# Gate and up: five units instead of three begin early, with the transposes of the third and fourth tiles of tokens behind them in TensorE's order

## The chip, the cores and the metric

One NeuronCore of one Trainium2 chip. The time is device microseconds of one execution of the whole kernel; the median of three runs of the kernel before was 1610.05 us (1607.22 to 1615.42). The traces name the engines PE (TensorE), DVE (VectorE), ACT (ScalarE), POOL (GpSimd) and SP (SyncE, which issues most DMAs).

## What is computed

The reference is a trunk of two layers over 512 tokens of width 1024 in float32. Layer 0 mixes tokens with a two-dimensional neighbourhood attention, layer 1 with three dilated attentions, merged by their softmax denominators. Each mixer, and each SwiGLU behind it, has a normalization ahead and one behind:

```
def swiglu(x, w_gate, w_up, w_down):
    return (jax.nn.silu(x @ w_gate) * (x @ w_up)) @ w_down

for layer in range(DEPTH):
    h = rms_norm(x, norm_mix_pre[layer])
    h = neighbourhood_attention(...) if layer % 2 == 0 else dilated_attention(...)
    x = x + rms_norm(h, norm_mix_post[layer])
    h = rms_norm(x, norm_ffn_pre[layer])
    x = x + rms_norm(swiglu(h, ...), norm_ffn_post[layer])
```

The hidden width of the SwiGLU is 2816: 22 blocks of 128 columns for gate and as many for up.

## The kernel before

Every float32 product is made of three matmuls of rounded halves (`mm3`: high by high L101, high by low L102, low by high L103). A `split` makes the two halves: ScalarE copies the high one (L89), VectorE subtracts to get the low one (L90). Such halves are called `h_a`, `l_a` and so on in the traces.

Large products save an eighth of their multiplications with a scheme of seven products instead of eight. The tokens (four tiles of 128) and the width are halved; seven operands are made of the quarters: X1A, X1B, D1, S2, S4, S3 and X2B. X1A and X1B hold tokens of tiles 0 and 1 alone. The other five need tiles 2 and 3 too: `operands` makes them on GpSimd with four sums a tile (L346, L348, L350, L352), and after each sum `transposed` sends 512 columns through TensorE (four transposes, L322) into one of two `t` banks, from where ScalarE copies the high half (L324) and VectorE subtracts the low half (L325). That L325 frees the bank. `tr_o1_2_3` is the operand 3 (D1) of tile 2 in layer 1; a tile's five transposes come in the order D1, S2, S4, S3, X2B (3, 4, 5, 6, 2).

Between attention and feed-forward stands `out_proj`: for each of the four tiles the output projection (`yo`), the normalization behind it (L359, L360, L306, L308, L366), the one ahead of the feed-forward (`prenorm`: L313, L304, L308 on GpSimd, L315 on VectorE), and the operands. X1A and X1B lie in `rxc`, the other five in `rxa`.

`gate_up` has 22 units, each one block of gate columns with one of up columns (class `Seven`): 84 matmuls of 128x256 into one bank, 12 for each of the seven products. A unit's `first` is the split of its weights a (`l_a`, from `r_gu` or, for units 2 to 4, from `fg`) and the products p1 (X1A) and p2 (X1B); p2's end also starts its `sink` (L558, L559). `third` makes weight sums (L168 and L169 on GpSimd, L170 and L174 on VectorE) and two more splits. `first` of units 0 to 2 is written ahead of the loop; in the loop `run` issues the steps of unit f, `third` of unit f + 1, and p1 and p2 of unit f + 3 in between. The partial gate of a unit is kept in `g_`, a ring of four buffers in the arena `fg`.

Order: a scheduler places the instructions of the whole program on each engine's queue by its own model of their durations; each engine then works strictly in that order and waits on semaphores. `after(i, j)` only forces i behind j on an engine, without a semaphore. So an edit in one place can reorder queues elsewhere. In the kernel before, the scheduler already draws p1 and p2 of units 3 and 4 ahead of unit 0's later products.

One more place matters: the end of the dilated attention. For each pair of heads j, `weights` exchanges softmax statistics between partitions through DRAM: `swapped` writes 8 KB or 4 KB (L919) and reads them back with four DMAs (L921), twice for a pair. Between the two, VectorE and ScalarE form the weights (exponential: L937). The weights scale 16 blocks of probabilities (L1032, eight for each half), which are then transposed (`t1_j`, L1046, copied out by L1047), multiplied with the values (`o1_j`), and enter the output projection. Scores are `sa_j` and `sb_j`, evicted by L953 on VectorE and L954 on ScalarE. SP's queue carries these small DMAs and the output projection's weights (`wo0` to `wo6`, two DMAs of 512 KB each).

Of the kernel before, what the change touches and what calls it, by code (L numbers as in the profile page):

```python
# [17 lines left out]
P = 128  # L18
SEQ = 512
D = 1024  # L20
# [18 lines left out]
def encoder_kernel(ctx: ExitStack, tc: tile.TileContext, a: dict, out: bass.AP):  # L39
    nc = tc.nc  # L40
# [65 lines left out]
    def after(i, j):  # L106

        tc.add_manual_dep(i.ins, j.ins.name,
                          mybir.DependencyInfo(mybir.DependencyClass.NoSync, mybir.DependencyReason.DATA),
                          reason="start flag")  # L110
# [17 lines left out]
    class Seven:  # L128
# [22 lines left out]
            self.i1 = prod(self.left, self.wa, 0, self.xs[X1A], True)  # L151

        def p2(self):
            after(prod(self.right, self.wa, 1, self.xs[X1B], False), self.i1)
            with tc.high_priority(self.urgent):
                self.sink(0, self.left, self.right)

                dve.memset(self.right, 0.0)
# [159 lines left out]
    def transposed(dst, src, name):  # L318

        p = bank("t", f"tr_{name}")  # L320
        for k in range(4):
            pe.transpose(p[:, k * P:(k + 1) * P], src[:, k * P:(k + 1) * P], ident)  # L322
        p3 = p.rearrange("p (k t) -> p k t", k=4)
        act.activation(dst[0], p3, AF.Copy)  # L324
        dve.tensor_sub(dst[1], p3, dst[0].bitcast(F32))  # L325

    def transposed_all(x, h, t, name):
        for hf in range(2):
# [2 lines left out]

    def operands(xs, x, hs, t, rcomb, name):

        def put(i, v):
            transposed(both(xs[i], ALL, ALL, slice(t % 2 * P, t % 2 * P + P)), v, f"{name}_{i}")

        ha, hb = hs[t][:, :512], hs[t][:, 512:]
        if x is not None:
            transposed_all(x, hs[t], t, name)
        elif t < 2:  # L340
            put(X1A, ha)
            put(X1B, hb)
        if t >= 2:
            h1a, h1b = hs[t - 2][:, :512], hs[t - 2][:, 512:]
            d1, s2 = next(rcomb), next(rcomb)
            pool.tensor_sub(d1, ha, hb)  # L346
            put(D1, d1)
            pool.tensor_sub(s2, d1, h1a)  # L348
            put(S2, s2)
            pool.tensor_add(h1b, s2, h1b)  # L350
            put(S4, h1b)
            pool.tensor_sub(h1a, h1a, ha)  # L352
            put(S3, h1a)
            if x is None:
                put(X2B, hb)

    def postnorm_half(hf, sq, y, g, name):
        m, s = small(f"ym{hf}_{name}"), slice(hf * 512, hf * 512 + 512)
# [136 lines left out]
    def out_proj(w, rv, layer, load_x, us, rings, gains):  # L495
        rbig, rhn, rcomb = rings
        g1 = gain(gains[0], a["g_mix_post"][layer])
        g2 = gain(gains[1], a["g_ffn_pre"][layer])
        us = [u for k in range(0, KD, 2) for u in units2(w[k:k + 2], f"wo{k}_{layer}", us[k:k + 2])]
        hs = {}  # L500

        def product(t):
            y = [bank(("pp", "pp", "s", "s", "pp", "o", "pp", "pp")[2 * t + hf], f"yo{layer}_{t}_{hf}")
                 for hf in range(2)]
            for k in range(KD):
                for hf in range(2):
                    mm3(y[hf], both(rv[k], ALL, block(t)), both(us[k], ALL, slice(hf * 512, hf * 512 + 512)),
                        k == 0, k == KD - 1)
            return y

        def post(t, y):
            x, hs[t] = next(rbig), next(rhn)
            load_x(x, t)
            postnorm(hs[t], y, g1, x, f"o{layer}_{t}")
            nc.sync.dma_start(spill[2 * layer][t], x)
            xs_[t] = x

        def pre(t):
            prenorm(hs[t], xs_[t], g2, f"o{layer}_{t}")

        def ops(t):
            operands(xs, None, hs, t, rcomb, f"o{layer}_{t}")

        xs_ = {}
        y0=product(0)
        y1=product(1)
        post(0,y0)
        post(1,y1)
        pre(0)
        pre(1)  # L530
        ops(0)
        ops(1)
        y=product(2)
        post(2,y)
        pre(2)
        y=product(3)
        ops(2)
        post(3,y)
        pre(3)
        ops(3)  # L540

    def gate_up(layer, xs, hid, fg):
        wg, wu = a["wg"], a["wu"]
        raws = ring(fg, 0, 2 * D, 3)
        g_, u_, p5_ = ring(fg, 6 * D, 512, 4), ring(fg, 8 * D, 512, 2), ring(fg, 9 * D, 256, 2)
        v_ = w22_ring(rxc[:, 4 * D:5 * D])
        units, us = {}, {}

        def unit_of(f):
            if f in units or f >= FT:  # L550
                return units.get(f)
            raw = load2((wg[layer, f], wu[layer, f]), f"gu{layer}_{f}", None if f % 5 < 2 else next(raws))
            b, g = bank(("s", "s", "pp", "o", "pp", "pp")[f % 6], f"gu{layer}_{f}"), next(g_)

            def sink(n, left, other):
                u = us.get(f)
                if n == 0:
                    act.activation(g[:, :256], other, AF.Copy)  # L558
                    dve.tensor_add(g[:, :256], g[:, :256], left)  # L559
                elif n == 1:  # L560
                    act.activation(u[:, :256], other, AF.Copy)
                    dve.tensor_sub(u[:, :256], u[:, :256], left)  # L562
                elif n == 2:
                    dve.tensor_sub(u[:, 256:], other, left)
                else:
                    act.activation(g[:, :256], g[:, :256], AF.Silu)
                    act.activation(g[:, 256:], left, AF.Silu)
                    dve.tensor_mul(hid[f], *(v.rearrange("p (h c) -> p h c", h=2) for v in (g, u)))

            units[f] = Seven(raw, b, xs, f"{layer}_{f}", sink, None, next(v_), (pool, pool, dve, dve))  # L570
            return units[f]

        ahead = 3
        for f in range(ahead):
            unit_of(f).first()
        for f in range(FT):
            for i in range(f, min(f + 2, FT)):
                if i not in us:
                    us[i], units[i].p5 = next(u_), next(p5_)
            run(unit_of(f), unit_of(f + 1), unit_of(f + ahead))  # L580

# [179 lines left out]
    def mix_out(layer, w, rxb, load_x):  # L763
        for j in range(PAIRS - 1):
            nc.gpsimd.dma_start(rxa[:, j * D:(j + 1) * D], rvd[layer][j])
        us = [None] * 4 + [hl(rxa, 8, D)] + [hl(rxb, 2 * i, D) for i in range(3)]
        with arena(f"ep{layer}", 12 * D, "right") as ep:
            out_proj(w, rv, layer, load_x, us, (ring(ep, 0, D, 4), ring(ep, 4 * D, D, 4), ring(ep, 8 * D, 512, 4)),
                     (ep[:, 10 * D:11 * D], ep[:, 11 * D:12 * D]))

    def ffn(layer, stack):
        hl_ = ring(rxc, 0, D, 5)
        rxb = None
        with arena(f"hid{layer}", FT * 512, "right") as hm:
            h2 = hm.rearrange("p (h x) -> p h x", h=2)
            hid = [h2[:, :, f * 256:f * 256 + 256] for f in range(FT)]
            with arena(f"fg{layer}", 9 * D + 512) as fg:
                gate_up(layer, xs, hid, fg)
            with arena(f"ed{layer}", D, "right") as ed, arena(f"yp{layer}", 2 * D, "right") as yp:
                rcomb = ring(ed, 0, 512, 2)  # L780

                def sink(t, xt, hs, gn):
                    if layer == 1:
                        for n in range(2 if t == NT - 1 else 1):
                            s = slice(512 * n, 512 * n + 512) if t == NT - 1 else ALL
                            (nc.sync, act)[n].dma_start(out[t][:, s], xt[:, s])
                    else:
                        nc.sync.dma_start(spill[1][t], xt)
                        prenorm(hs[t], xt, gn, f"n{layer}_{t}")
                        operands(mixer_operands(rxb) if rxb is not None else None, x, hs, t, rcomb, f"n{layer}_{t}")  # L790

                with arena(f"wd{layer}", 2 * QF) as mem, arena(f"raw{layer}", 2 * D) as more:
                    end = down(layer, hm, hl_, mem, yp, more, sink)
                if layer == 0:
                    rxb = stack.enter_context(arena("rxb1", 6 * D, dtype=F32R))
                end()
        return rxb
# [66 lines left out]
             lambda v: v.rearrange("p (i c) -> p c i", i=ROWS))  # L864

    inner.close()
    mix_out(0, a["na_o"], rxb, lambda xt, t: nc.sync.dma_start(xt, a["x_rows"][t]))
    stack.close()
    rxb = ffn(0, stack)

# [255 lines left out]
                nc.sync.dma_start(xt[32 * r + 16:32 * r + 32], rows[r, 0:16])  # L1128

    inner.close()  # L1130
    mix_out(1, a["dil_o"], rxb, load_block)
    stack.close()
    ffn(1, stack)


def _blocks(w, cols):
# [79 lines left out]
```

## Time and profile before

| | us |
|---|---|
| median of three runs | 1610.05 |
| the profiled execution, its time | 1605.1 |
| its span in the trace | 1603.3 |
| TensorE busy | 1486.7 |
| VectorE busy | 1205.0 |
| ScalarE busy | 897.6 |
| GpSimd busy | 628.1 |

The granted clock of TensorE was 0.976 on the mean. A row of waits reads: engine, line and tile that waited, what released it, microseconds in total, times, the longest. A row of a timeline reads: start, duration, engine, line, operation, tile out <- tiles in, shapes, count, and in brackets the idle time before it with what ended it. A row of stretches reads: from and to, length, then the busy time of PE, weight loads, DVE, ACT and POOL with the number of instructions, the granted clock, the DMA share and GB/s. A row of DMAs reads: what, queue, number, KB each, microseconds from issue to landing.

### The profile page before, as it was taken

The page shows a single profiled execution, that of the slowest core. Times are in us where ns is not written, and L with a number is a line of the kernel's source. Part 1 is how long each engine was busy: PE and PEld are TensorE (multiplying, and loading weights), DVE is VectorE, ACT ScalarE, POOL GpSimd, SP SyncE. Part 2 cuts the span into 40 slices and gives each one's busy share as a digit, 9 for nine tenths or more (in the row PEclk, how much of TensorE's full clock was granted, in tenths as well). Part 3 has the DMA queues.
Part 4 walks back from the last instruction along what each step waited for, and adds up shares of the span by engine and source line. Part 5 has one row for each costly group of instructions (what it writes and reads, how often), then busy time and mean ns, then how long its engine had stood idle before and what let it go on. Part 6 is the DMA issues. An engine that isn't in the chain of part 4 may idle for free.

```text
span 1603.3 us, 28068 instructions
## 1 busy us (share of the span) xinstructions
PE 1486.7 (93%) x10788; PEld 1366.7 (85%) x10788; DVE 1205.0 (75%) x1884; ACT 897.6 (56%) x1787; POOL 628.1 (39%) x500
## 2 busy tenths in 40 slices
PE   7999898899999898889999999999887899999896
PEld 7988776899999786879999988988766899999774
DVE  5488966799998867677677776776536699998866
ACT  5367753555555556434467776676654555555554
POOL 3356434533330222566555443544104533330221
PEclk9999999999999999999999999999998999999999
DMA  4323455133323995534322322322626133323993
GB/s 171 109 80 105 150 191 197 66 106 106 106 80 99 256 243 172 173 132 159 109 95 62 121 81 92 133 67 61 222 88 197 66 106 106 106 80 102 265 244 112
DMA packets 77766, 208.99 MB, mean 130 GB/s; under 512 B 18560, under 2 KB 28800, under 8 KB 77632
## 3 DMA queue, kind: packets, MB, share of 16 engines
q1 hardware_dynamic: 65456, 165.11, 30.5%
q0 software_dynamic: 12032, 41.82, 10.9%
q8 instruction: 85, 1.39, 0.4%
q14 instruction: 49, 0.40, 0.1%
q10 hardware_dynamic: 144, 0.26, 0.0%
HBM read 185.04 MB, written 22.12 MB: 129 GB/s over the span
## 4 chain that ended last, share of the span: by engine, by line
PE 61%; DVE 12%; DMA 11%; issue 6%; ACT 5%; POOL 4%; SPq 1%; POOLq 0%; DVEq 0%; ACTq 0%
PE gu L101 9%; PE gu L102 9%; PE gu L103 9%; PE pp_d L101 4%; PE pp_d L102 3%; PE pp_d L103 3%; DMA raw<-wd 3%; DMA wd<-wd 2%; PE t L1046 2%; PE sb L986 1%; ACT ap L1032 1%; PE vd L102 1%; PE vd L101 1%; PE vd L103 1%; PE yd_pp L101 1%
## 5 line engine op out<-in xcount | busy, mean ns | idle before, releaser
L103 PE MATMUL gu<-rxc,l_a 128*128 128x256 f32 x352 | 102.0, 290 | 3.3 <-DVE l_a L90 3.3
L102 PE MATMUL gu<-rxc,h_a 128*128 128x256 f32 x352 | 102.4, 291 | 0.0
L101 PE MATMUL gu<-rxc,h_a 128*128 128x256 f32 x352 | 102.1, 292 | 0.1
L101 PE MATMUL gu<-rxa,h_c 128*128 128x256 f32 x352 | 100.2, 285 | 0.7 <-DVE fg L562 0.4
L101 PE MATMUL gu<-rxa,h_b 128*128 128x256 f32 x352 | 99.7, 284 | 0.7 <-ACT rxa L324 0.7
L102 PE MATMUL gu<-rxa,h_b 128*128 128x256 f32 x352 | 99.8, 284 | 0.0
L103 PE MATMUL gu<-rxa,l_c 128*128 128x256 f32 x352 | 99.6, 283 | 0.0
L102 PE MATMUL gu<-rxa,h_c 128*128 128x256 f32 x352 | 99.6, 283 | 0.0
L103 PE MATMUL gu<-rxa,l_b 128*128 128x256 f32 x352 | 99.5, 283 | 0.0
L604 POOL DMA_DIRECT2D wd<-wd x36 | 34.3, 995 | 137.8 <-DVE l_d0p L90 49.7
L168 POOL TENSOR_TENSOR fg<-fg 128x512 f32<-128x512 f32 x24 | 39.8, 1659 | 120.9 <-DVE l_a L90 119.7
L954 ACT ACTIVATE ap<-ap 128x256 f32<-128x256 f32 x128 | 63.9, 502 | 31.4 <-DVE ap L953 30.8
L168 POOL TENSOR_TENSOR r_d<-r_d 128x512 f32<-128x512 f32 x24 | 39.7, 1656 | 105.9 <-DVE l_ad L90 97.7
L168 POOL TENSOR_TENSOR r_gu<-r_gu 128x512 f32<-128x512 f32 x20 | 35.5, 1773 | 115.8 <-DVE l_a L90 115.8
L89 ACT ACTIVATE rxc<-hid 128x512 fp32r<-128x512 f32 (+1 forms) x84 | 49.2, 591 | 54.1 <-PE yd_s L102 33.6
L103 PEld LDWEIGHTS gu<-rxc,l_a 128*128 128x128 f32 x352 | 70.0, 199 | 3.7 <-DVE l_a L90 3.7
L101 PEld LDWEIGHTS gu<-rxc,h_a 128*128 128x128 f32 x352 | 69.8, 199 | 0.6 <-ACT rxc L324 0.6
L102 PEld LDWEIGHTS gu<-rxc,h_a 128*128 128x128 f32 x352 | 70.0, 199 | 0.0
L101 PEld LDWEIGHTS gu<-rxa,h_c 128*128 128x128 f32 x352 | 67.5, 192 | 1.7 <-DVE fg L562 1.5
L101 PEld LDWEIGHTS gu<-rxa,h_b 128*128 128x128 f32 x352 | 67.6, 193 | 1.0 <-ACT rxa L324 1.0
L102 PEld LDWEIGHTS gu<-rxa,h_c 128*128 128x128 f32 x352 | 67.5, 192 | 0.2
L103 PEld LDWEIGHTS gu<-rxa,l_b 128*128 128x128 f32 x352 | 67.6, 192 | 0.0
(599 smaller groups left out, 6265.2 us busy)
## 6 DMA issues: line engine op xcount, KB each, us to landing
r_d<-dil_qk SPq DMA_DIRECT2D x48, 512.0 KB, 4.5
r_d<-wd SPq DMA_DIRECT2D x30, 512.0 KB, 4.4
wd<-wd POOLq DMA_DIRECT2D x30, 512.0 KB, 10.4
fg<-wg SPq DMA_DIRECT2D x24, 512.0 KB, 3.7
fg<-wu SPq DMA_DIRECT2D x24, 512.0 KB, 4.6
r_gu<-wg SPq DMA_DIRECT2D x20, 512.0 KB, 3.7
r_gu<-wu SPq DMA_DIRECT2D x20, 512.0 KB, 4.6
r_n<-na_qk SPq DMA_DIRECT2D x16, 512.0 KB, 4.5
```

Source lines behind the costliest of these rows:

```text
L89: act.activation(h, src, AF.Copy)
L101: i = pe.matmul(o, s[0], m[0], start=start, stop=False, skip_group_check=True)
L102: pe.matmul(o, s[0], m[1], start=False, stop=False, skip_group_check=True)
L103: pe.matmul(o, s[1], m[0], start=False, stop=stop, skip_group_check=True)
L168: e[0].tensor_add(q[0], q[0], q[2])
L604: nc.gpsimd.dma_start(v, src, accum_op=ALU.add)
L954: act.activation(pr[:, f], pr[:, f], AF.Exp, bias=st[:, c:c + 1], scale=-1.0, accum_out=st[:, c + 2:c + 3])
L986: pe.matmul(ss[hd][:, f0:f0 + P], qf[rw, block(c)], kf[rw, block(c)], start=True, stop=True)
L1032: act.activation(v, v, AF.Copy, scale=w[:, 2 * b + hd:2 * b + hd + 1])
L1046: pe.transpose(t[:, block(i)], part(a_b, *blocks[4 * n + i]), ident)
```

## The change

`first` of five units instead of three is written ahead of the loop, and the loop starts a later unit only from unit 5 on. `operands` returns the first transpose of each operand, and `gate_up` forces those of tile 2 behind the start of unit 1's second product and those of tile 3 behind that of unit 4. The ring `g_` has five buffers, and the arena is 512 columns wider. The returned lists are passed through `out_proj`, `mix_out` and `ffn`.

```diff
         def p2(self):
-            after(prod(self.right, self.wa, 1, self.xs[X1B], False), self.i1)
+            self.i2 = prod(self.right, self.wa, 1, self.xs[X1B], False)
+            after(self.i2, self.i1)
...
         for k in range(4):
-            pe.transpose(p[:, k * P:(k + 1) * P], src[:, k * P:(k + 1) * P], ident)
+            i = pe.transpose(p[:, k * P:(k + 1) * P], src[:, k * P:(k + 1) * P], ident)
+            first = i if k == 0 else first
...
+        return first
...
+        trs = []
+
         def put(i, v):
-            transposed(both(xs[i], ALL, ALL, slice(t % 2 * P, t % 2 * P + P)), v, f"{name}_{i}")
+            trs.append(transposed(both(xs[i], ALL, ALL, slice(t % 2 * P, t % 2 * P + P)), v, f"{name}_{i}"))
...
         y=product(3)
-        ops(2)
-        post(3,y)
+        trs = ops(2)
+        post(3, y)
         pre(3)
-        ops(3)
-
-    def gate_up(layer, xs, hid, fg):
+        return trs, ops(3)
+
+    def gate_up(layer, xs, hid, fg, trs):
         wg, wu = a["wg"], a["wu"]
         raws = ring(fg, 0, 2 * D, 3)
-        g_, u_, p5_ = ring(fg, 6 * D, 512, 4), ring(fg, 8 * D, 512, 2), ring(fg, 9 * D, 256, 2)
+        g_, u_, p5_ = ring(fg, 6 * D, 512, 5), ring(fg, 8 * D + 512, 512, 2), ring(fg, 9 * D + 512, 256, 2)
...
-        ahead = 3
-        for f in range(ahead):
+
+
+        ahead, early = 3, 5
+        for f in range(early):
             unit_of(f).first()
+        for f, v in zip((1, early - 1), trs):
+            for tr in v:
+                after(tr, units[f].i2)
         for f in range(FT):
...
-            run(unit_of(f), unit_of(f + 1), unit_of(f + ahead))
+            run(unit_of(f), unit_of(f + 1), unit_of(f + ahead) if f + ahead >= early else None)
...
-            with arena(f"fg{layer}", 9 * D + 512) as fg:
-                gate_up(layer, xs, hid, fg)
+            with arena(f"fg{layer}", 10 * D) as fg:
+                gate_up(layer, xs, hid, fg, trs)
```

How the queues stand then, at the places of which the prediction speaks. Lines of the changed kernel are a few higher for the same operation (L168 becomes L169, L346 to L352 become L351 to L357, L325 becomes L327, L937 becomes L948, L1032 becomes L1043).

On TensorE, layer 0 changes little: the first transposes of tile 2 move behind 12 matmuls each of units 0 and 1, and those of tile 3 by a few matmuls. In layer 1 tile 2's first and second transposes move behind 35 matmuls of units 0 and 1, and the third of tile 2 behind all of unit 2; the 22 matmuls of unit 4 that stood between the third and fourth transposes of tile 3 now stand ahead of them.

GpSimd's queue at the change to the feed-forward in layer 1, before (`fg1` are the weight sums of units 2 to 4, two for each unit; `rs_o1_3` is tile 3's factor in the normalization; `ep1` the sums for tile 3's operands):

```order
L168 TENSOR_TENSOR fg1_12636<-fg1_12636 128x512
L169 TENSOR_TENSOR fg1_12636<-fg1_12636 128x512
L308 TENSOR_TENSOR rs_o1_3_12585<-v_o1_3_12583,mhalf_71 128x1
L346 TENSOR_TENSOR ep1_12186<-ep1_12186 128x512
L168 TENSOR_TENSOR fg1_12636<-fg1_12636 128x512
L348 TENSOR_TENSOR ep1_12186<-ep1_12186 128x512
L169 TENSOR_TENSOR fg1_12636<-fg1_12636 128x512
L350 TENSOR_TENSOR ep1_12186<-ep1_12186 128x512
L352 TENSOR_TENSOR ep1_12186<-ep1_12186 128x512
```

and now:

```order
L169 TENSOR_TENSOR fg1_12636<-fg1_12636 128x512
L309 TENSOR_TENSOR rs_o1_3_12585<-v_o1_3_12583,mhalf_71 128x1
L170 TENSOR_TENSOR fg1_12636<-fg1_12636 128x512
L169 TENSOR_TENSOR fg1_12636<-fg1_12636 128x512
L351 TENSOR_TENSOR ep1_12186<-ep1_12186 128x512
L170 TENSOR_TENSOR fg1_12636<-fg1_12636 128x512
L169 TENSOR_TENSOR fg1_12636<-fg1_12636 128x512
L353 TENSOR_TENSOR ep1_12186<-ep1_12186 128x512
L170 TENSOR_TENSOR fg1_12636<-fg1_12636 128x512
L355 TENSOR_TENSOR ep1_12186<-ep1_12186 128x512
L357 TENSOR_TENSOR ep1_12186<-ep1_12186 128x512
```

Unit 4's two sums, which stood behind all of tile 3's, now stand ahead of the third. In layer 0 the same two move in, and one sum of unit 3 goes ahead of tile 3's factor.

VectorE's queue there, now (before, `l_b1_0` and the two L325 of tile 2 stood ahead of L315, and unit 4's split far behind it):

```order
L372 SCALAR_TENSOR_TENSOR ep1_12186<-ep1_12186,rs_yo1_3_12577 128x1024
L90 TENSOR_TENSOR l_a1_2_12711<-fg1_12636,h_a1_2_12710 128x1024
L305 TENSOR_SCALAR v_o1_3_12583<-m_o1_3_12581 128x1
L90 TENSOR_TENSOR l_a1_3_12745<-fg1_12636,h_a1_3_12744 128x1024
L316 SCALAR_TENSOR_TENSOR ep1_12186<-ep1_12186,rs_o1_3_12585 128x1024
L90 TENSOR_TENSOR l_a1_4_12779<-fg1_12636,h_a1_4_12778 128x1024
L565 TENSOR_TENSOR fg1_12636<-fg1_12636,gu1_0_12640 128x256
L327 TENSOR_TENSOR rxa_76<-tr_o1_2_3_12527,rxa_76 128x4x128
L327 TENSOR_TENSOR rxa_76<-tr_o1_2_4_12535,rxa_76 128x4x128
```

The splits of units 3 and 4 moved ahead, and the subtractions that free the banks of tile 2's first transposes moved behind them.

SP's queue at the end of the dilated attention, before (`sw0` and `sw2` are pair 6's two swaps, `r_wo2_1` to `r_wo6_1` the output projection's weights):

```order
L919 DMA sw0_6472<-ap1_6470 128x16
L85 DMA r_wo2_1_12200<-dil_o 128x1024 x2
L921 DMA ap1_6470<-sw0_6472 32x4x4 x4
L919 DMA sw2_6474<-ap1_6470 128x8
L921 DMA ap1_6470<-sw2_6474 32x4x2 x4
L85 DMA r_wo4_1_12211<-dil_o 128x1024 x2
```

and now:

```order
L85 DMA r_wo2_1_12200<-dil_o 128x1024 x2
L930 DMA sw0_6472<-ap1_6470 128x16
L932 DMA ap1_6470<-sw0_6472 32x4x4 x4
L85 DMA r_wo4_1_12211<-dil_o 128x1024 x2
L930 DMA sw2_6474<-ap1_6470 128x8
L932 DMA ap1_6470<-sw2_6474 32x4x2 x4
```

Each of the two weight loads moved ahead of the small write of its swap. On ScalarE the exponential of pair 6's weights and both groups of eight scalings moved behind splits of the output projection's weights, and the second group behind two copies of pair 7's queries (L425 and L426 before).

More of the change, by code (lines that the diff above doesn't have):

```diff
@@ L355, in operands @@
                 put(X2B, hb)
+        return trs
     def postnorm_half(hf, sq, y, g, name):
@@ L521, in ops @@
         def ops(t):
-            operands(xs, None, hs, t, rcomb, f"o{layer}_{t}")
+            return operands(xs, None, hs, t, rcomb, f"o{layer}_{t}")
         xs_ = {}
@@ L767, in mix_out, with ffn @@
         with arena(f"ep{layer}", 12 * D, "right") as ep:
-            out_proj(w, rv, layer, load_x, us, (ring(ep, 0, D, 4), ring(ep, 4 * D, D, 4), ring(ep, 8 * D, 512, 4)),
+            return out_proj(w, rv, layer, load_x, us, (ring(ep, 0, D, 4), ring(ep, 4 * D, D, 4), ring(ep, 8 * D, 512, 4)),
                      (ep[:, 10 * D:11 * D], ep[:, 11 * D:12 * D]))
-    def ffn(layer, stack):
+    def ffn(layer, stack, trs):
         hl_ = ring(rxc, 0, D, 5)
@@ L866, in encoder_kernel @@
     inner.close()
-    mix_out(0, a["na_o"], rxb, lambda xt, t: nc.sync.dma_start(xt, a["x_rows"][t]))
+    trs = mix_out(0, a["na_o"], rxb, lambda xt, t: nc.sync.dma_start(xt, a["x_rows"][t]))
     stack.close()
-    rxb = ffn(0, stack)
+    rxb = ffn(0, stack, trs)
     ap = inner.enter_context(arena("ap1", 14 * D + 3264, "right"))
@@ L1130, in encoder_kernel @@
     inner.close()
-    mix_out(1, a["dil_o"], rxb, load_block)
+    trs = mix_out(1, a["dil_o"], rxb, load_block)
     stack.close()
-    ffn(1, stack)
+    ffn(1, stack, trs)
 def _blocks(w, cols):
```

## The prediction

> **What bounds the kernel now.** I read the page first, then TensorE's busy time in stretches, then its waits at the two changes from attention to feed-forward, then the rows there.
>
> ```profile
> span 1603.3 us, 28068 instructions
> PE 1486.7 (93%) x10788; PEld 1366.7 (85%) x10788; DVE 1205.0 (75%) x1884; ACT 897.6 (56%) x1787; POOL 628.1 (39%) x500
> 250.00:312.00 62.00, 50.20 (x311) 44.78 (x310) 47.17 (x59) 30.40 (x58) 38.72 (x26) 0.92 0.41 156
> 350.00:400.00 50.00, 50.00 (x419) 50.00 (x418) 46.58 (x59) 25.77 (x44) 16.32 (x9) 1.00 0.32 106
> 1150.00:1190.00 40.00, 37.35 (x233) 30.24 (x232) 22.46 (x62) 23.70 (x62) 4.66 (x6) 1.00 0.45 155
> 1222.00:1275.00 53.00, 40.46 (x274) 37.72 (x272) 38.70 (x52) 26.27 (x47) 35.47 (x23) 0.87 0.37 136
> ```
>
> TensorE is busy 93% of the span. In the steady part of gate and up (350 to 400) it is busy 50.00 of 50.00 us: a fifth gate buffer and a different interleaving of units can gain nothing there. At the change to the feed-forward it is idle 62.00 - 50.20 = 11.8 us in layer 0 and 53.00 - 40.46 = 12.5 us in layer 1. Only those are there to be won. They split up so (first layer 0, then layer 1):
>
> ```profile
> PE tr_o L322 <- DVE rxc L325: 6.1, 2, 3.5
> PE gu L103 <- DVE l_a L90: 3.3, 2, 2.9
> PE tr_o L322 <- DVE rxa L325: 1.6, 3, 1.0
> ...
> PE tr_o L322 <- DVE rxc L325: 7.7, 2, 4.3
> PE tr_o L322 <- POOL ep L350: 2.8, 1, 2.8
> PE tr_o L322 <- POOL ep L348: 1.4, 1, 1.4
> PE tr_o L322 <- DVE rxa L325: 0.4, 1, 0.4
> ```
>
> The larger halves, 6.1 and 7.7 us, are waits for VectorE to finish the operands of tiles 0 and 1 (rxc is X1A and X1B). Their two parts are the one before tile 1's own transposes and the one before the first transposes of tile 2. In layer 0 the rest hangs on a weight split (l_a), in layer 1 on GpSimd's sums for tile 3.
>
> **The change, part by part.** *The first transposes of tile 2 go behind unit 1's second product.* The wait that stands before them:
>
> ```profile
> 277.42 1.09 PE L322 MATMUL tr_o<-ident,ep 128*128 128x128 f32 x4 [3.55 <-DVE rxc L325]
> 1238.88 1.09 PE L322 MATMUL tr_o<-ident,ep 128*128 128x128 f32 x4 [3.41 <-DVE rxc L325]
> 1238.06 1.27 DVE L325 TENSOR_TENSOR rxc<-tr_o,rxc 128x512 fp32r<-128x512 f32 x2
> ```
>
> What takes their place is gate and up's L102, high weights times the low half of X1A, and the low half of tile 1 is written by the same L325: 1238.06 plus half of 1.27 is 1238.7. So 3.55 and 3.41 us of wait stay, under another name. The gain is four transposes that no longer run at the slow clock, 1.09 against 0.60 us when warm: at most 0.5 us a layer, and I count it as 0, since the same four are paid for later.
>
> *Unit 4's products and splits come earlier, tile 3's chain later (layer 0).* What can go there is the wait for unit 4's split:
>
> ```profile
> 297.68 0.58 PE L103 MATMUL gu<-rxc,l_a 128*128 128x256 f32 x1 [2.88 <-DVE l_a L90]
> 301.87 1.03 PE L322 MATMUL tr_o<-ident,ep 128*128 128x128 f32 x8
> 288.67 2.20 POOL L346 TENSOR_TENSOR ep<-ep 128x512 f32<-128x512 f32 x1 [1.40 <-DVE ep L315]
> 290.83 2.28 POOL L168 TENSOR_TENSOR fg<-fg 128x512 f32<-128x512 f32 x1
> 293.06 1.28 POOL L348 TENSOR_TENSOR ep<-ep 128x512 f32<-128x512 f32 x1
> 294.29 2.25 POOL L169 TENSOR_TENSOR fg<-fg 128x512 f32<-128x512 f32 x1
> 296.51 2.26 POOL L350 TENSOR_TENSOR ep<-ep 128x512 f32<-128x512 f32 x1
> ```
>
> Removing it would bring TensorE to tile 3's second and third transposes (301.87) 2.9 us earlier, at 299.0. But they need L348 and L350, and GpSimd now does one weight add (L168 of unit 3) before tile 3's rstd, and unit 3's L169 and unit 4's L168 and L169 before L348. Of these, L168 and L169 of unit 3 already stood before L350; unit 4's two are new in front of it. Two adds at 1.28 to 2.28 us move L350's end from 298.77 to between 301.3 and 303.3. The earlier matmuls then wait there: the layer 0 sum is between -2.0 (the adds fill the 1.40 us idle before L346: 301.3 - 1.4 = 299.9) and +1.5 (303.3 against 301.87). I take 0, between ends nearly alike.
>
> *The same in layer 1.* Here the order really puts tile 3's transposes behind unit 4, where 22 of its matmuls stood between the third and the fourth.
>
> ```profile
> 1246.70 1.29 POOL L169 TENSOR_TENSOR fg<-fg 128x512 f32<-128x512 f32 x1
> 1249.90 2.20 POOL L346 TENSOR_TENSOR ep<-ep 128x512 f32<-128x512 f32 x1 [1.40 <-DVE ep L315]
> 1252.06 2.42 POOL L168 TENSOR_TENSOR fg<-fg 128x512 f32<-128x512 f32 x1
> 1256.77 1.27 POOL L169 TENSOR_TENSOR fg<-fg 128x512 f32<-128x512 f32 x1
> 1258.00 2.28 POOL L350 TENSOR_TENSOR ep<-ep 128x512 f32<-128x512 f32 x1
> 1260.33 1.12 PE L322 MATMUL tr_o<-ident,ep 128*128 128x128 f32 x4 [2.81 <-POOL ep L350]
> 1265.38 0.60 PE L322 MATMUL tr_o<-ident,ep 128*128 128x128 f32 x4
> ```
>
> GpSimd does unit 4's two adds before L350 too, 2 x 1.27 = 2.5 to 2.42 + 2.25 = 4.7 us, less the 1.40 us that it idled before L346 where that can be used: L350 ends 1.1 to 4.7 us later. I take 4.2, near the slow end, because VectorE's queue now holds the two-input operations L366, three l_a splits and L315 in a row, with the L325 of tile 2 behind them, and GpSimd's adds beside such operations are the ones of 2.2 to 2.4. So tile 3's third transposes move from 1260.33 to 1264.5, the fourth need L352 (one more such add of 1.27, so 1265.8) and start 0.4 later than the 1265.38 of before, although 22 fewer matmuls lie between. Behind an idle stretch the clock is low:
>
> ```profile
> 1261.00:1264.00 3.00, 3.00 (x18) 3.00 (x17) 0.96 (x2) 0.90 (x2) 2.92 (x3) 0.57 0.02 5
> ```
>
> 18 matmuls in 3.0 us, 0.167 each at a granted clock of 0.57, against 50.00 / 419 = 0.119 when warm. The slow stretch now falls on some 12 to 20 matmuls behind the transposes as it fell on others before, but later by the same shift: about +1. The term is +1.5, between -3 (GpSimd not later, 22 matmuls ahead of it) and +4. Before that a new wait stands at tile 2's third transposes: the L325 that frees their bank is behind L315, l_a of unit 4 and L559. It is hidden by the later one as long as it is under some 3 us.
>
> The Trainium skill, "SBUF — State Buffer", section "Who interferes with whom", says that a VectorE operation with two SBUF inputs and a GpSimd operation that reads SBUF block each other for a whole instruction. The trace agrees: 1.27 alone, 2.42 beside such work. By that rule every added pair costs its full length, L350 would be 4.7 late and this term +2.0 instead of +1.5; if the rule did not hold, -3.
>
> *The end of the dilated attention (layer 1) is ordered anew too.* The diff does not touch it, but the scheduler does. On SP's queue the loads of wo2 and wo4 (1 MB each) now stand before the small writes that start the two swaps of pair 6's softmax weights; on ScalarE the exponential of these weights (L937) moves behind two weight splits, and both scalings (L1032, eight each) behind it, the second behind the copies L425 and L426.
>
> ```profile
> ap<-sw SPq DMA_DIRECT2D x4, 2.0 KB, 5.7
> ap<-sw SPq DMA_DIRECT2D x4, 1.0 KB, 1.7
> sw<-ap SPq DMA_DIRECT2D x1, 4.0 KB, 1.4
> 1148.06 9.12 SPq L85 DMA_DIRECT2D r_wo<-dil_o  x4
> 1149.70 3.30 ACT L1032 ACTIVATE ap<-ap 128x256 f32<-128x256 f32 x8
> 1157.96 0.63 ACT L426 ACTIVATE rxc<-ap 64x512 fp32r<-64x512 f32 x1
> 1155.42 0.66 PE L1046 MATMUL t<-ident,ap 128*128 128x128 f32 x4 [1.95 <-ACT ap L1047]
> ```
>
> The first swap's read-back stood behind 1 MB and took 5.7 us; the second's, with nothing ahead, 1.7. So 1 MB ahead costs 4.0. For the first swap the load moves from behind its write to ahead of it: no change. For the second, wo4 (issued at 1148.06, behind it) now stands ahead: +4.0. The second eight scalings, 3.30 us, now follow L426 instead of running before 1153: +3.3. Together pair 6's transposes are 7.3 later. TensorE's order puts 33 output-projection matmuls ahead of all but the first of them, but these are taken from behind, where they covered the evictions of pair 7's scores (between its second and third block of scores stood 18, now none). Cover is moved, not made; TensorE has 40.00 - 37.35 = 2.65 us of idle time in this stretch that moved work could fill, half of it say: 7.3 - 1.3 = 6.0. The bounds are 0 (the 33 matmuls cover all) and 7.3. Pair 7's swaps follow the evictions, and the last output projection waits for pair 7, so the delay comes out at the end.
>
> *The rest* (one more ring buffer, a wider arena, returned lists) issues nothing. The weight loads of units 2 to 4 stand where they stood on SP's queue.
>
> **Sum:** 0 + 1.5 + 6.0 = +7.5. On the profiled execution 1605.1 + 7.5 = 1612.6; the median of the runs shown is 4.95 above that execution, so 1610.05 + 7.5 = 1617.5 us.
>
> **Rivals.** *The change does what it says* (faster): the waits on POOL and on l_a go, 3.3 in layer 0 and 4.2 in layer 1, with 0.5 a layer for warm transposes, and the tail's new order costs nothing since the 33 matmuls cover it: 1610.05 - 8.5 = 1601.5. For it: TensorE has all of units 3 and 4 ahead of tile 3. Against: GpSimd's queue, which these waits end on, only got longer. Chance 0.22.
>
> *Nothing but shifting* (within the bound): layer 1 gives back what it gains and the tail is half covered, 0 + 0 + 3 = 1613. For it: no work is added, and TensorE has filler in each place. Against: the filler in each place is taken from another. Chance 0.32.
>
> *The same losses, larger* is part of my forecast: tail 7.3, layer 1 +4 and layer 0 +1.5 give 1622.9.
>
> The clock makes a rival of size, not of sign: after 2.81 us of waiting in layer 1 the granted clock was 0.57. The Trainium skill, "TensorE: Matmul & The Clock Gate", section "What's actually happening", has the clock halved after an idle window of some 3.4 us. By it, new waits shorter than that would leave the clock high and layer 1 would cost about 1 less; the trace is harsher than that.
>
> **How the numbers follow.** My forecast, slower by about 5 to 13 us, has 0.46; the rivals 0.32 and 0.22. A measurement of this kernel tells about 0.5%, 8.05 us, from no change. My sum of 7.5 lies just under that, with a long side above it (12.8 with the terms' upper ends), and the profile shows no term that would hold the loss down, while the middle case and the lower part of mine fall within the bound: slower 0.46, same 0.32, faster 0.22. The range takes in the faster case down to about 7 us and the larger losses with 6 us for a place that I did not see: 1603 to 1629; mine alone, 1614 to 1624.
>
> **What would show it.** In the changed kernel: TensorE's wait of about 3.4 us on L325 before gate and up's second matmul (first step); tile 3's transposes in layer 0 waiting for L350 with l_a's 2.88 gone; L350 in layer 1 later by 1 to 5 us measured from unit 0's first matmul, and a new wait at tile 2's third transposes; pair 6's second swap with a landing of over 5 us, and more than 2.65 us of TensorE idle between pair 6's and pair 7's scores. I am wrong if steady gate and up is no longer at 50 of 50, if the tail's idle time is as before, or if L348 and L350 end no later.

## The result, and the profile after

| | us |
|---|---|
| kernel before, median of 12 runs | 1608.84 (1605.40 to 1615.42) |
| changed kernel, median of 12 runs | 1609.99 (1606.67 to 1615.12) |
| ratio, 95% interval | 1.0004 (0.9992 to 1.0016) |
| profiled execution of the changed kernel, span | 1607.5 |

The change makes no difference that can be measured; the interval reaches from 1.3 us faster to 2.6 us slower. Forecast was +7.5.

TensorE's busy time of the changed kernel in the same four stretches as before:

```profile
250.00:312.00 62.00, 51.93 (x305) 46.43 (x304) 49.88 (x61) 30.65 (x59) 39.61 (x26) 0.86 0.43 165
350.00:400.00 50.00, 50.00 (x419) 50.00 (x418) 43.67 (x57) 25.66 (x46) 16.64 (x11) 1.00 0.31 106
1150.00:1190.00 40.00, 35.52 (x207) 28.52 (x207) 19.08 (x56) 24.06 (x64) 3.39 (x6) 0.96 0.42 133
1222.00:1275.00 53.00, 40.31 (x259) 36.99 (x258) 40.93 (x49) 24.61 (x44) 36.25 (x23) 0.84 0.34 129
```

The steady part is full as before. At the change in layer 0 TensorE is busy 1.73 us more than before (51.93 against 50.20), and yet does 305 matmuls in place of 311: the column behind the counts of GpSimd, the granted clock, fell from 0.92 to 0.86. Busy time rose because the same work ran slower. Its waits there, first layer 0 (245 to 330), then layer 1 (1222 to 1330):

```profile
PE tr_o L323 <- DVE rxa L327: 4.6, 3, 3.6
PE gu L102 <- DVE rxc L327: 3.2, 1, 3.2
PE tr_o L323 <- DVE rxc L327: 2.3, 1, 2.3
...
PE tr_o L323 <- DVE rxa L327: 4.8, 4, 2.2
PE gu L102 <- DVE rxc L327: 3.8, 1, 3.8
PE tr_o L323 <- DVE rxc L327: 3.7, 1, 3.7
```

Most of the waiting that the change was to end has come back under another name. The wait on l_a (3.3) is gone in layer 0, and the transposes wait 4.6 for the L327 that frees their bank, against 1.6 before. The waits on GpSimd (4.2) are gone in layer 1, and there too 4.8 stand at the banks, against 0.4. The wait for X1A went from the transposes to `gu L102`, about as long as before (3.2 and 3.8 against 3.55 and 3.41).

To compare without the rest of the program I take the stretch from unit 0's first matmul to the end of gate and up's last in one profile. For the changed kernel's layer 1 it is read so:

```profile
1233.40 0.80 PE L101 MATMUL gu<-rxc,h_a 128*128 128x256 f32 x2
...
1485.18 0.28 PE L103 MATMUL gu<-rxa,l_c 128*128 128x256 f32 x1
```

1485.46 - 1233.40 = 252.06 us. The tail of attention is read from layer 1's first output-projection matmul to unit 0's first. All kernels, in us:

| kernel | layer 0 | tail | layer 1 | ratio of times, 95% interval |
|---|---|---|---|---|
| before | 250.21 | 99.33 | 249.12 | 1 |
| changed | 250.16 | 99.38 | 252.06 | 1.0004 (0.9992 to 1.0016) |
| e1: five gate buffers alone | 250.19 | 99.27 | 248.64 | 1.0007 (0.9994 to 1.0019) |
| e2: change in layer 1 alone | 250.72 | 100.20 | 250.82 | 1.0020 (1.0006 to 1.0034) |
| e3: change in layer 0 alone | 250.61 | 100.02 | 249.71 | 1.0007 (0.9995 to 1.0018) |
| e4: tile 2's place alone | 249.92 | 99.20 | 251.12 | 1.0018 (1.0005 to 1.0031) |
| e5: five units early, no place forced | 250.17 | 98.65 | 246.62 | 0.9992 (0.9978 to 1.0006) |
| e9: early, tile 3's place forced | 250.32 | 99.45 | 248.69 | 0.9992 (0.9977 to 1.0007) |
| e6: GpSimd's sums of units 2 on behind | 248.08 | 96.46 | 247.78 | 0.9991 (0.9980 to 1.0003) |
| e8: the sums of units 3 on behind | 250.16 | 98.99 | 245.68 | 0.9982 (0.9970 to 0.9994) |
| e7: change, with e6's sums | 247.79 | 99.52 | 248.35 | 0.9983 (0.9969 to 0.9997) |
| e10: e5 with e6's sums | 247.84 | 97.93 | 245.49 | 0.9957 (0.9942 to 0.9972) |
| e11: e5 with e8's sums | 248.45 | 98.48 | 248.20 | 0.9985 (0.9972 to 0.9999) |

A ratio compares many runs of a kernel with runs of the kernel before beside them; a stretch is read from one profile. How exact a stretch is can be seen where TensorE's order is the same to a matmul or two: layer 0 differs by 0.5 us (e1 and e2), layer 1 by 1.1 (e1 and e3) and 1.2 (changed and e2), the tail by 2.9 (before and e6).

### The profile page after: what moved, and what is told of

It reads as the page before. It is cut to its first block, busy times and chain, and to the rows that moved or that the text cites. A ratio compares the mean times of both kernels' runs of the same rounds, so it can differ in the third digit from the quotient of the medians.

```text
span 1607.5 us, 28077 instructions
## 1 busy us (share of the span) xinstructions
PE 1491.8 (93%) x10788; PEld 1371.3 (85%) x10788; DVE 1189.5 (74%) x1884; ACT 895.8 (56%) x1787; POOL 609.8 (38%) x500
## 4 chain that ended last, share of the span: by engine, by line
PE 59%; DVE 12%; DMA 11%; issue 7%; ACT 5%; POOL 4%; SPq 1%; POOLq 0%; DVEq 0%; ACTq 0%
PE gu L101 9%; PE gu L102 9%; PE gu L103 9%; PE pp_d L101 4%; PE pp_d L102 3%; PE pp_d L103 3%; DMA wd<-wd 2%; PE t L1057 2%; DMA r_d<-wd 2%; DMA raw<-wd 1%; PE sb L997 1%; PE vd L102 1%; ACT ap L1043 1%; PE yd_pp L101 1%; PE yd_pp L102 1%
## 5 line engine op out<-in xcount | busy, mean ns | idle before, releaser
L102 PE MATMUL gu<-rxc,h_a 128*128 128x256 f32 x352 | 102.3, 291 | 7.0 <-DVE rxc L327 7.0
L102 PE MATMUL gu<-rxa,h_b 128*128 128x256 f32 x352 | 101.3, 288 | 0.0
L102 PE MATMUL gu<-rxa,h_c 128*128 128x256 f32 x352 | 99.6, 283 | 0.0
L169 POOL TENSOR_TENSOR fg<-fg 128x512 f32<-128x512 f32 x24 | 36.0, 1500 | 121.8 <-DVE l_a L90 120.6
L169 POOL TENSOR_TENSOR r_d<-r_d 128x512 f32<-128x512 f32 x24 | 39.8, 1658 | 104.8 <-DVE l_ad L90 96.4
L169 POOL TENSOR_TENSOR r_gu<-r_gu 128x512 f32<-128x512 f32 x20 | 29.4, 1470 | 128.9 <-DVE l_a L90 128.9
L102 PEld LDWEIGHTS gu<-rxc,h_a 128*128 128x128 f32 x352 | 69.8, 198 | 7.5 <-DVE rxc L327 7.5
L101 PEld LDWEIGHTS gu<-rxa,h_b 128*128 128x128 f32 x352 | 68.9, 196 | 0.7 <-ACT rxa L326 0.7
L102 PEld LDWEIGHTS gu<-rxa,h_b 128*128 128x128 f32 x352 | 69.0, 196 | 0.0
L101 PEld LDWEIGHTS gu<-rxa,h_c 128*128 128x128 f32 x352 | 67.5, 192 | 1.1 <-DVE fg L568 0.9
```

The costliest lines, as they stand in the source:

```text
L101: i = pe.matmul(o, s[0], m[0], start=start, stop=False, skip_group_check=True)
L102: pe.matmul(o, s[0], m[1], start=False, stop=False, skip_group_check=True)
L169: e[0].tensor_add(q[0], q[0], q[2])
```

## The experiments

**e1, the tail by itself.** Five buffers alone make the scheduler reorder the end of the dilated attention as in the changed kernel (SP's queue is the same; some of pair 7's scores and of pair 6's transposes stand a little elsewhere). Both changes to the feed-forward stay as they were within a matmul; later, where TensorE is full, the units interleave otherwise.

```diff
-        g_, u_, p5_ = ring(fg, 6 * D, 512, 4), ring(fg, 8 * D, 512, 2), ring(fg, 9 * D, 256, 2)
+        g_, u_, p5_ = ring(fg, 6 * D, 512, 5), ring(fg, 8 * D + 512, 512, 2), ring(fg, 9 * D + 512, 256, 2)
...
-            with arena(f"fg{layer}", 9 * D + 512) as fg:
+            with arena(f"fg{layer}", 10 * D) as fg:
```

> The kernel before with five gate buffers instead of four and the wider arena, nothing else. Its queues at both changes to the feed-forward stand within one matmul as before, but the end of the dilated attention is ordered as in the changed kernel (wo2 and wo4 ahead of the small swap writes, L1032 later). So it prices that tail alone. By the prediction's term the tail costs 6.0 us, between 0 and 7.3: ratio 1.0037. By the theory formed from the changed kernel's trace the output projection's matmuls, drawn ahead, cover the later transposes, and the second swap is not later at all: 0 within 1.5 us, ratio 0.999 to 1.001, and TensorE's waits from 1110 to 1222 us sum to within 1.5 us of the 10.3 us of before.

The tail took 99.27 us against 99.33. The ratio is the stronger evidence: 1.0007, with 1.0019 or 3.1 us as its upper end, so 6.0 us is ruled out. TensorE's waits between 1110 and 1222 us, before and in e1:

```profile
PE t L1046 <- ACT ap L1032: 2.7, 1, 2.7
PE yo L101 <- ACT h_wo L89: 2.0, 1, 2.0
PE t L1046 <- ACT ap L1047: 1.9, 1, 1.9
PE sb L986 <- ACT ap L412: 1.3, 1, 1.3
```

```profile
PE t L1046 <- ACT ap L1032: 4.5, 2, 2.6
PE pp_d L101 <- DVE ap L409: 1.3, 1, 1.3
PE yo L101 <- DVE ap L953: 0.9, 1, 0.9
...
PE sa L969 <- DVE ap L953: 0.5, 1, 0.5
```

With the smaller rows 10.3 us became 9.1. The later scalings cost a new wait of 2.6 on L1032 at pair 6's transposes, while pair 7's shrank from 2.7 to 2.0 (4.5 - 2.7 = 1.8 in all), the scores 0.5; the wait on wo0's split (2.0) is gone, and that on pair 6's copies shrank from 1.9 to 0.2.

**e2 and e3, one layer each.**

```diff
-        ahead, early = 3, 5
+        ahead, early = 3, 5 if layer == 1 else 3
...
-        for f, v in zip((1, early - 1), trs):
+        for f, v in zip((1, early - 1), trs if layer == 1 else ()):
```

> The change in layer 1 alone (layer 0 starts three units early, no transposes forced). If layer 1's change to the feed-forward costs about 3 us, as one profile showed (2.9 from unit 0's first matmul to the last of gate and up), the ratio is 1.001 to 1.003 and that stretch is 251 to 253 us against 249.1 before. If the 2.9 was a variation of one profile, the stretch is 249 to 250. The prediction's term was +1.5.

> The change in layer 0 alone. By the prediction's term and the trace of the changed kernel layer 0 is worth 0: the stretch from unit 0's first matmul to the last of gate and up stays 250.2 us within 0.5, ratio 0.999 to 1.001 (the tail's order is the new one too). If the change itself gains there and something else gave it back, the stretch is 2 to 3 us shorter.

Layer 1 alone: 250.82 us, slower by 1.7 than before, and the only half whose time is slower beyond its interval (1.0006 to 1.0034); the changed kernel, with the same layer 1, is not (1.0004). 250.82 is just under the 251 expected, so the 2.9 of the first profile was partly its own. Layer 0 alone: 250.61, nothing beyond the 0.5 that equal orders differ by.

**e4, e5 and e9, the change in its parts.** e4 forces only tile 2's transposes behind unit 1, with three early units:

```diff
-        ahead, early = 3, 5
+        ahead, early = 3, 3
...
-        for f, v in zip((1, early - 1), trs):
-            for tr in v:
-                after(tr, units[f].i2)
+        for tr in trs[0]:
+            after(tr, units[1].i2)
```

> Only tile 2's transposes forced behind unit 1's second product, three units early as before, nothing for tile 3. GpSimd's queue then does not have unit 4's sums ahead of tile 3's third. If the loss in layer 1 comes from pushing tile 2's transposes (their banks are freed late behind L315 and the splits on VectorE), the stretch of layer 1 is 251 to 253 us here too. If it comes from unit 4's earlier splits and sums on VectorE and GpSimd, it is 248 to 249.5.

e5 has five early units and forces nothing; e9 forces only tile 3's transposes:

```diff
-        for f, v in zip((1, early - 1), trs):
-            for tr in v:
-                after(tr, units[f].i2)
```

```diff
-        for f, v in zip((1, early - 1), trs):
-            for tr in v:
-                after(tr, units[f].i2)
+        for tr in trs[1]:
+            after(tr, units[early - 1].i2)
```

> Five units begin early and the ring has five buffers, but no transpose is forced behind anything. Unit 4's splits and sums stand early on VectorE and GpSimd as in the change; in layer 1 tile 2's transposes stay about where they were. If layer 1's loss is the forced place of tile 2's transposes (e4 lost 2.0 with that alone), the stretch of layer 1 from unit 0's first matmul to the last of gate and up is 249 to 250 us and the ratio 0.999 to 1.001. If it is the earlier splits and sums, the stretch is 251 to 253 and the ratio about 1.002.

> The change without the forced place of tile 2's transposes; tile 3's stay forced behind unit 4. If layer 1's loss is tile 2's place alone, layer 1's stretch is 246 to 248 us as in e5 (246.6) and the ratio 0.998 to 1.000. If tile 3's place counts too, it lies between e5's 246.6 and the changed kernel's 252.1, at 249 or more.

In layer 1 tile 2's forced place alone costs 2.0 us (e4, 251.12 against 249.12), five early units alone win 2.5 (e5, 246.62), which is more than either theory gave them; tile 3's place gives 2.1 of that back (e9, 248.69, between the two expectations, and less than twice the 1.2 that equal orders differ by), tile 2's the rest (changed, 252.06, and e2, 250.82). In layer 0 none of the parts moves anything. In e5 layer 1 looks so:

```profile
1249.41 0.60 PE L323 MATMUL tr_o<-ident,ep 128*128 128x128 f32 x4
1251.03 0.60 PE L323 MATMUL tr_o<-ident,ep 128*128 128x128 f32 x4
1256.01 0.63 PE L323 MATMUL tr_o<-ident,ep 128*128 128x128 f32 x4 [1.41 <-DVE rxa L327]
...
1265.66 0.66 PE L323 MATMUL tr_o<-ident,ep 128*128 128x128 f32 x4 [0.16 <-POOL ep L355]
1268.15 0.63 PE L323 MATMUL tr_o<-ident,ep 128*128 128x128 f32 x4 [1.42 <-DVE rxa L327]
```

and in the changed kernel so:

```profile
1252.04 0.63 PE L323 MATMUL tr_o<-ident,ep 128*128 128x128 f32 x4 [1.48 <-DVE rxa L327]
...
1261.59 1.30 PE L323 MATMUL tr_o<-ident,ep 128*128 128x128 f32 x8 [2.15 <-DVE rxa L327]
1263.16 0.51 PE L101 MATMUL gu<-rxa,h_b 128*128 128x256 f32 x2 [0.26 <-ACT rxa L326]
1264.68 1.09 PE L323 MATMUL tr_o<-ident,ep 128*128 128x128 f32 x4 [1.02 <-DVE rxa L327]
```

In e5 one operand's transposes follow the last after 1.6 to 5 us of other work, and two waits of 1.4 are left. In the changed kernel they stand closer together at the end of the early units, and 2.15, 0.26 and 1.02 us of waiting come within 5.3 us. What ended the 2.15 is seen on VectorE:

```profile
1258.42 1.71 DVE L90 TENSOR_TENSOR l_b<-r_gu,h_b 128x1024 fp32r<-128x1024 f32 x1
...
1260.77 1.35 DVE L327 TENSOR_TENSOR rxa<-tr_o,rxa 128x512 fp32r<-128x512 f32 x2
```

The transposes of 1257.64 lay in their bank, but the L327 that frees it stood behind a weight split and ran at 1260.77. So the bank waited for VectorE's queue. Whether it is the crowding of the transposes or the place of the splits on VectorE that costs more is not tested apart.

**e6 and e8, GpSimd's queue alone.** The kernel before, with one order more: the weight sums of later units behind tile 3's last sum.

```diff
         def sums(self):
             ...
-            e[0].tensor_add(q[0], q[0], q[2])
+            i = e[0].tensor_add(q[0], q[0], q[2])
+            if self.behind is not None:
+                after(i, self.behind)
...
-            pool.tensor_sub(h1a, h1a, ha)
+            last = pool.tensor_sub(h1a, h1a, ha)
...
             units[f] = Seven(raw, b, xs, f"{layer}_{f}", sink, None, next(v_), (pool, pool, dve, dve))
+            units[f].behind = last if f >= 2 else None
```

`last` is handed on to `gate_up`; e8 has `f >= 3`.

> The kernel before, with GpSimd's weight sums of units 2 and later forced behind tile 3's four sums; nothing else, the old tail included. If GpSimd's queue is what TensorE waits for in layer 1 (1.4 and 2.8 us on L348 and L350), these waits go and the stretch of layer 1 falls from 249.1 to 245 to 247.5; in layer 0, where no wait is put on GpSimd, it stays within 1 us of 250.2 unless VectorE gets faster beside an idle GpSimd. Ratio 0.997 to 0.999. If something else comes last right behind (VectorE's L325, its splits), the waits change their name and the ratio is 1.000.

> As e6, but unit 2's sums stay ahead of tile 3's; its TensorE order is that of the kernel before to the row. Tile 3's third sum then starts one L168 and one L169 sooner (2.4 and 1.3 us): waits on GpSimd in layer 1 fall from 4.2 to 1 or less, ratio 0.998 to 1.000.

e8, whose TensorE order in both changes to the feed-forward is that of before, wins 3.4 us in layer 1 (245.68), and its ratio of 0.9982 is clear of 1. Its waits there:

```profile
PE tr_o L325 <- DVE rxc L328: 7.7, 2, 4.3
PE tr_o L325 <- DVE rxa L328: 2.2, 3, 1.3
```

Waits on GpSimd are gone; 1.8 of the 4.2 came back at the banks (2.2 against 0.4). e6 wins 2.1 in layer 0, where its expectation allowed 1 unless VectorE got faster, and 1.3 in layer 1, less than expected and hardly more than equal orders differ by: with its other TensorE order there unit 4's split comes last (2.1).

**e7, e10 and e11, the two together.** e7 adds e6's order to the changed kernel; e10 adds it to e5, and e11 adds e8's to e5.

> The changed kernel with the same sums forced behind tile 3's. If the change's early units are worth something once GpSimd's queue is out of the way, layer 0's stretch is 2 to 3 us under 250.2 and layer 1's 2 to 4 us under the 252.1 of the changed kernel, ratio 0.997 to 0.999. If the forced place of tile 2's transposes is the loss, layer 1 stays at 251 or more whatever GpSimd does.

> e5 (five units early, nothing forced on TensorE) with GpSimd's sums of units 2 and later behind tile 3's. If the two gains add, layer 0's stretch is about 248 us (as e6, e7) and layer 1's 244 to 246, ratio 0.996 to 0.998. If they are the same gain twice, layer 1 stays at 246 to 247.5.

> As e10 with unit 2's sums left ahead of tile 3's. Layer 0's stretch 247.5 to 250 us, layer 1's 244 to 246.5, ratio 0.996 to 0.999; by the other theory (the same gain twice) layer 1 is not under e8's 245.7 and the ratio not under e8's 0.9982.

In layer 0 the 2.4 us of e7 and e10 (247.8 against 250.2) come with GpSimd's order; e6 has 2.1 of them without early units, but by another way. In the first 50 us e6 waits 0.5 less at a higher clock (0.93 against 0.90), e7 3.5 less at a lower one (0.85).

In layer 1 it is not shown that the two gains add. For it: e10, at 245.49, is under e5 (246.62) and e6 (247.78). Against: e8's order alone gives as much (245.68), and e11 came out as "the same gain twice" had it, not under e8 in layer 1 (248.20, 1.7 over its expectation) nor in the ratio (0.9985). There the change with e6's order reaches 248.35, under the 251 that a loss by tile 2's place alone would have left, and 2.9 us over e10, which has no forced places. e10 is the best kernel of all: 0.9957 (0.9942 to 0.9972), some 7 us faster than before, where e5 and e6 alone are not clear of 1; 1.4 of the 7 lie in the tail of its profile, which these orders do not touch. e6's short tail (96.46), whose order there is that of before, is not explained. GpSimd's queue in e10, layer 1:

```profile
1245.24 1.30 POOL L354 TENSOR_TENSOR ep<-ep 128x512 f32<-128x512 f32 x1 [1.40 <-DVE ep L319]
1246.62 2.17 POOL L356 TENSOR_TENSOR ep<-ep 128x512 f32<-128x512 f32 x1
1248.87 2.16 POOL L358 TENSOR_TENSOR ep<-ep 128x512 f32<-128x512 f32 x1
1250.99 1.28 POOL L360 TENSOR_TENSOR ep<-ep 128x512 f32<-128x512 f32 x1
1252.24 5.74 POOL L170 TENSOR_TENSOR fg<-fg 128x512 f32<-128x512 f32 x3
```

Tile 3's third sum ends at 1251.03, 19.5 us after unit 0's first matmul (1231.54), where before it ended 25.6 after (1260.28 - 1234.68), and in the changed kernel 27.85.

## Why the prediction was wrong

The range held the time (1609.99 in 1603 to 1629), the forecast, slower by 7.5 us, did not come. With the tail's 6.0 put at the 0 that was found, the sum would be +1.5; the medians differ by 1.2.

- *First transposes of tile 2, 0 expected*: right. The wait went to `gu L102`, 3.2 and 3.8 us.
- *Layer 0, 0 expected*: right in size, 250.16 against 250.21. GpSimd's third sum for tile 3 ended 27.5 us after unit 0's first matmul against 25.4, later by 2.1; the term had 2.6 to 4.6 less up to 1.4 of idle time. The 0 was luck in part, because the transposes did not come to wait for GpSimd: what came last was the L327 that frees the bank (3.55 us ahead of tile 3's second). And the gain went into the clock. In the 50 us from unit 0's first matmul the waits fell from 9.3 to 8.0 us, the granted clock fell too, and the same 302 matmuls were done:

```profile
273.35:323.35 50.00, 40.66 (x302) 38.99 (x303) 39.23 (x51) 24.55 (x40) 29.29 (x18) 0.90 0.26 97
```

```profile
274.54:324.54 50.00, 41.97 (x302) 40.41 (x301) 41.59 (x53) 24.80 (x42) 29.81 (x18) 0.83 0.26 99
```

- *Layer 1, +1.5 expected (between -3 and +4)*: +2.9 in the changed kernel and +1.7 in e2, so the size was about right, in part by luck, and the cause partly wrong. L350's counterpart ended 2.25 us later by the same count, where 4.2 was taken. But TensorE no longer waited for GpSimd: tile 3's third transposes came 3.2 us later, 1.0 after their sum was ready; the new wait at tile 2's third transposes (1.48) was seen, and called hidden, and those behind it at the other banks were not seen. The same 50 us hold 9.1 us of waits in place of 8.2, at a clock of 0.83 in place of 0.88.
- *The tail, "7.3 - 1.3 = 6.0"*: this is the step that failed; e1 measures it at 0 (the ratio allows 1.0 us less to 3.1 more). The first part was wrong; the second was right in size, but the step from it to the time was not. The swap: "1 MB ahead costs 4.0" took wo4's load to be issued when it was before. In the changed kernel:

```profile
1142.56 0.86 SPq L85 DMA_DIRECT2D r_wo<-dil_o  x2
1146.47 0.33 SPq L930 DMA_DIRECT2D sw<-ap  x1
1147.89 1.75 SPq L932 DMA_DIRECT2D ap<-sw  x4
```

The load goes out 5.5 us sooner than at 1148.06, and the swap's write comes 3.9 us behind it. The load's halves landed 3.6 and 4.4 us after they were issued, the second 1 us after the write went out, yet the write took 1.4 us as before. The landings of both swaps, with the first swap's write before in the first row:

```profile
sw<-ap SPq DMA_DIRECT2D x1, 8.0 KB, 2.5
...
ap<-sw SPq DMA_DIRECT2D x4, 2.0 KB, 1.7
ap<-sw SPq DMA_DIRECT2D x4, 1.0 KB, 1.8
sw<-ap SPq DMA_DIRECT2D x1, 8.0 KB, 6.2
sw<-ap SPq DMA_DIRECT2D x1, 4.0 KB, 1.4
```

The first swap's "no change" held in its sum: its write behind 1 MB took 6.2 us in place of 2.5, its read-back 1.7 in place of 5.7. The load ahead of the second swap can go out sooner because another move, which the term did not follow, emptied its buffer sooner. Before, the buffer was empty at 1146.07, 1.3 us after the swap's write had gone out at 1144.81, and SP's queue held the load until behind the read-back. With its place on SP's queue alone changed, the load and the write behind it would have had to wait for the buffer. wo4 takes the buffer that wo0's splits empty, and the second of these stood behind L937, which before waited 7.72 us for the first swap. Now it stands ahead of it, and the buffer is empty at 1142.15:

```profile
1143.65 0.21 ACT L937 ACTIVATE ap<-ap 128x16 f32<-128x16 f32 x1 [7.72 <-DVE ap L936]
1143.77 1.04 ACT L89 ACTIVATE h_wo<-r_wo 128x1024 fp32r<-128x1024 f32 x1
```

```profile
1139.84 1.06 ACT L89 ACTIVATE h_wo<-r_wo 128x1024 fp32r<-128x1024 f32 x1 [5.11 <-issue]
...
1145.31 0.22 ACT L948 ACTIVATE ap<-ap 128x16 f32<-128x16 f32 x1 [1.92 <-DVE ap L947]
...
1152.57 3.30 ACT L1043 ACTIVATE ap<-ap 128x256 f32<-128x256 f32 x8
```

The scalings: the second eight did come 2.9 us later (1152.57 against 1149.70; 3.3 expected), but "cover is moved, not made" did not hold. Pair 6's transposes did wait 2.6 us for them in e1, but waits ahead of that, 2.0 on wo0's split and most of the 1.9 on pair 6's copies, went, and where the 33 matmuls were missing, between pair 7's scores, only 0.5 us of wait showed (`sa <- L953` in e1). A lower bound of 0 had been given for exactly this, and the value taken near the upper one. ScalarE was done with pair 7's scores at 1181.58 us against 1181.43 before, and pair 7's swaps follow them.

Of the signs that were named, the wait at L102, the later third sum and the wait at tile 2's third transposes came; the second swap's landing of over 5 us did not. TensorE's idle time between pair 6's and pair 7's scores rose as foretold (40.00 - 35.52 = 4.5 us against 2.65), and still the tail was no longer. Over the whole of 1110 to 1222 us the waits sum to 9.7 us against 10.3, so idle time in one part of the tail was the wrong sign.

Of the rivals, "nothing but shifting" is nearest to the time, though its sum of +3 is just above the interval. Its reason, filler in each place, holds for the tail. The changes to the feed-forward shift too: waits from GpSimd and splits to banks, with the clock taking the rest.

The loss in layer 1 can be split. Over the whole stretch TensorE was idle for 9.15 us in place of 8.40 and busy for 242.91 in place of 240.72, so of the 2.9 us 0.7 are waits and 2.2 slower running. The granted clock shows the second part. In these stretches it is 1.00 or 0.50 in every profile, and it stays low for 3.41 us or for two or three times as long; so one such step costs some 1.7 us, by an estimate from half of 3.41. Between 20 and 40 us after unit 0's first matmul layer 1 has two low steps in the changed kernel and in e3, none in e5, e6, e8 and e10, and one in the others. The first, before:

```profile
1260.15:1263.57 3.42, 3.24 (x15) 3.24 (x16) 0.96 (x2) 0.90 (x2) 3.34 (x4) 0.50 0.02 5
```

One step more or less also goes with the 1.1 us between e1 and e3, and the 1.2 between changed and e2, whose orders are the same to a matmul or two. And e11, with e10's order of TensorE to the matmul, is idle 1.3 us longer (1.64 of it new, at tile 2's fourth transposes) and busy 1.4 us longer, with one low step where e10 has none.

What stays open: what makes the clock fall in one profile and not in another of the same order, and why VectorE frees that bank later in e11.

## What to carry to other kernels

Before an order is forced on one engine, look at what empties the buffers that the moved work needs, and where that stands in its own queue: here transposes waited for two banks, and VectorE freed one of them only behind a weight split. When the waits of an engine name another engine's queue, try to reorder that queue first; one order more on GpSimd (e8) was worth more than the whole change. And when a queue is reordered, price the new order by when its entries can start now, not by their old times: a load moved ahead of a small transfer cost nothing, because the buffer that it needed came free sooner too.

## What was not expected of the hardware

The granted clock fell after several short waits close together as after one long one. In the changed kernel, layer 1, after a single wait of 1.48 us and after 2.15, 0.26 and 1.02 us between 1259.4 and 1264.7:

```profile
1252.10:1255.00 2.90, 2.90 (x25) 2.88 (x26) 2.72 (x5) 1.08 (x3) 2.90 (x2) 1.00 0.00 0
...
1260.43:1263.84 3.41, 1.76 (x10) 1.14 (x10) 3.03 (x6) 3.09 (x6) 2.06 (x2) 1.00 0.14 58
1263.84:1267.25 3.41, 2.57 (x12) 2.60 (x13) 2.26 (x5) 1.01 (x2) 0.00 (x0) 0.50 0.76 231
1267.25:1270.67 3.42, 3.42 (x18) 3.42 (x17) 0.00 (x0) 0.17 (x1) 0.00 (x0) 0.50 0.21 81
```

25 matmuls in 2.90 us at a clock of 1.00, later 18 in 3.42 us at 0.50. In e5 the waits of 1.41 and 1.42 us, 12 us apart, left the clock at 1.00. The Trainium skill, "TensorE: Matmul & The Clock Gate", section "What's actually happening", gives an idle window of some 3.4 us for the drop; none of these waits was that long, so the drop fits it only if the window need not be idle throughout. The rows show that it need not: in the 3.41 us ahead of the drop TensorE was busy for 1.76 us, with 10 matmuls. How little work lets the clock fall they do not settle: in e2, after much the same waits, it stayed low for 3.41 us in place of 6.83.
